# A planner's assumptions about landings, and where range checks may stand, in a one-core streaming encoder step

## The chip, the cores and the metric

The kernel runs on one core of a Trainium2 chip. A core has five engines that work side by side, each through its own instructions in a fixed order: TensorE (PE; its weight loads are shown apart as PEld) multiplies matrices, VectorE (DVE) and ScalarE (ACT) work elementwise, GpSimd (POOL) does the same more slowly, and SyncE (SP) issues DMAs. GpSimd also issues DMAs here. Instructions of different engines wait for each other through semaphores. The metric is the device time of one execution in microseconds.

## The reference, cut to what matters

One layer of an encoder is computed for 1024 tokens of a prompt and 8 x 16 sample tokens, 1152 tokens in all, with shared weights. From each token's normalised and modulated state `h` (width 1024) one wide projection makes everything else:

```python
mod = jax.nn.silu(c) @ w_ada + b_ada
shift, scale, gate = jnp.split(mod[:, None, :], 3, axis=-1)
h = rms_norm(x, norm_g) * (1 + scale) + shift
proj = h @ w_in
q, k, v, z_att, z_ssd, xbc, dt_raw, gates = jnp.split(proj, IN_SPLITS, axis=-1)
...
att_branch = (o_att.reshape(b, s, ATT_WIDTH) * jax.nn.silu(z_att)) @ w_att_proj
...
ssd_branch = y @ w_ssd_proj
g_att, g_ssd = jnp.split(gates, 2, axis=-1)
merged = jax.nn.sigmoid(g_att) * att_branch + jax.nn.sigmoid(g_ssd) * ssd_branch
out = x + gate * (merged @ w_out)
```

Branch A is attention over the own chunk of 64 and the 8 before it, branch B a gated state-space scan (SSD) over chunks of 64 with a short convolution ahead. Everything is float32.

## The kernel before, in words

**Precision.** Each float32 operand of a large product is split into two float16 halves: the high half is the rounded value, the low half what the rounding lost. A product is three float16 matmuls (high x high, high x low, low x high). `halves` (L691 to L698) does the split of a weight: ScalarE writes the high half (L697), VectorE the low half (L698). `level` (L685 to L689) is the range check of an operand: ScalarE squares it into a scratch tile and keeps the row means (L689, followed by a short read of the accumulator). Near the end `verdict` looks at these sums; its result decides whether the general kernel that follows in the program has to run (with these inputs it does not). So a range check has no reader for a long time, but it reads the raw weight, and the raw buffer cannot be loaded again before.

**Weights.** A weight piece of 512 KB (128 x 1024) is loaded by SyncE into one of three raw buffers (`w_ahead`, L675 to L681, the DMA is L679), rounded, checked, and its buffer is freed. `w_split` (L749) does this for one piece of a plain job, `quad_split` (L715) for one piece of a quad job. The projections of the last stage are quad jobs: the product of 2 x 2 blocks is made from seven products instead of eight (`quad_dense`), from four pieces. Two of them are input blocks (`in_quad_dram`), two are sums of blocks that `quad_sums` made earlier and stored in device memory (`sum_d`). Twenty quad jobs follow each other at the end.

**Stages.** 0 to about 58 us: norm, modulation, `h`, and the first projection. All of it is written out by hand: each instruction is `late`, which pins it behind the one before it on its engine. To about 600 us: attention, head pair by head pair, with the projections (`dense_tok` L1023 to L1025, `dense` L970 to L973) as filler for TensorE. To about 1265 us: the SSD scan with its projections. After that: the merge and the quad products (L876 to L878, evicted by L895 and L901, with conversions L2198 and L2200 of their operands).

**What sets the order.** The Python code writes instructions into a list. The class `Order` then plans an order for each engine, which the program keeps. It groups up to three matmuls to a unit, finds what each unit depends on, and simulates the five engines with assumed costs. At each step it takes the engine that can go on first, and on it, of the units that can start, the one earliest in the list, with two preferences. A unit is "sure" when its inputs have been there for a margin (300 ns on ScalarE and VectorE, 2500 ns after a DMA); sure ones go first. And a unit in the set `fill` counts as 600 places later in the list. A unit in `pinned` keeps its place behind its predecessor. The assumed landing of a DMA is in these lines (L386 to L388): `bus` is the end of the transfers so far, `lat` first the bytes by 360 GB/s (1456 ns for 512 KB), and at the end the time from issue to landing; a reader can start 60 ns after it.

```python
bus = max(t + 1400, bus) + lat
lanes[e][k] = bus + 700
lat = bus + 700 - t
```

Nothing in the plan is a clock on the chip: it only fixes the order, and on the chip each engine waits where an input is not there.

**Where the range checks of the first part stand.** `level(wraw[0].ap, SW, late)` (L1257), the three `level(b.ap, SW, late)` in `w_low2` (L1233), and the eight of `h` in `h_level` (L1437), which are neither pinned nor in `fill`.

Of the kernel before, what the change touches and what calls it, by code (L numbers as in the profile page):

```python
# [136 lines left out]
        self.arena.release(self.at)  # L137


class Order:  # L140


# [6 lines left out]
    FAST = 300  # L149
    SAFE_FAST = 200.0  # L150

    def __init__(self, tc, instructions, pinned, cuts, slow, fill, fast):
        self.tc, self.slow, self.fill, self.fast = tc, slow, fill, fast
        self.list = [x for x in instructions if x.opcode != "TilePoolBoundary"]
        self.pinned, self.cuts = pinned, cuts

    @staticmethod
    def engine(x):
# [74 lines left out]
    def build(self):  # L233

        units, self.of, last = [], {}, None
        for x in self.list:
            e = self.engine(x)
            if e == "PE":
                small = x.tile_size[0] * x.tile_size[1] < 16384
                out = x.outs[0].bass_ap.tensor.name  # L240
                key = (small, tuple(x.tile_size), "" if small else out)
                if last and last["key"] == key and x.name not in self.cuts and (small or len(last["ins"]) < 3):
                    last["ins"].append(x)
                    self.of[x.name] = last
                    continue
            u = {"eng": e, "ins": [x], "i": len(units), "pred": {}, "succ": [], "key": None}
            if e == "PE":
                u["key"] = key
                last = u
            units.append(u)  # L250
            self.of[x.name] = u
        self.units = units

        hist, prev = {}, {}
        tiles = {}
        for x in self.list:
            u = self.of[x.name]
            e = u["eng"]
            if x.name in self.pinned and e in prev and prev[e] is not u:
                u["pred"].setdefault(prev[e]["i"], 0)  # L260
            prev[e] = u
            acc = [(a, False) for a in x.ins if hasattr(a, "bass_ap")] + [(a, True) for a in x.outs if hasattr(a, "bass_ap")]
            for a, w in acc:
                t, name, r0, r1, c0, c1 = self.region(a)
                if not w and name.startswith("in_"):
                    continue
                tag = name.rstrip("0123456789_") if "PSUM" in str(t.space) else None
                if tag in self.SLOTS:
                    tiles.setdefault(name, [tag, []])[1].append(u["i"])
                    r0, r1, c0, c1, w = 0, 128, 0, 512, True  # L270
                for blk in range(c0 // 512, (c1 - 1) // 512 + 1):
                    h = hist.setdefault((name, blk), [])
                    keep = []
                    for v in h:
                        q0, q1, d0, d1, j, jw = v
                        if q0 < r1 and r0 < q1 and d0 < c1 and c0 < d1 and (w or jw):
                            if j != u["i"]:
                                k = 2 if jw and not w else 1
                                u["pred"][j] = max(u["pred"].get(j, 0), k)
                            if w and r0 <= q0 and q1 <= r1 and c0 <= d0 and d1 <= c1:  # L280
                                continue
                        keep.append(v)
                    b0, b1 = max(c0, 512 * blk), min(c1, 512 * blk + 512)
                    new = (r0, r1, b0, b1, u["i"], w)
                    if not keep or keep[-1] != new:
                        keep.append(new)
                    hist[name, blk] = keep
        for u in units:
            costs = [self.cost(x) for x in u["ins"]]
            u["busy"] = sum(c for c, _ in costs)  # L290
            u["fast"] = u["ins"][0].name in self.fast
            u["at"] = u["i"] + self.FILL * (u["ins"][0].name in self.fill) - self.FAST * u["fast"]
            u["lat"] = u["busy"] - costs[-1][0] + costs[-1][1]
            u["dma"] = u["ins"][0].opcode == "DMACopy" or u["ins"][0].opcode.startswith("DmaTranspose")
        self.tiles = tiles
        opener, members = {}, {}
        for name, (tag, us) in tiles.items():
            us = sorted(set(us))
            first = units[us[0]]
            first.setdefault("opens", []).append(name)  # L300
            if opener.get(tag, us[0]) != us[0]:
                first["pred"].setdefault(opener[tag], 0)
            opener[tag] = us[0]
            for j in us:
                units[j].setdefault("uses", []).append(name)
            members[name] = tag, us
            tiles[name] = [tag, len(us), 0.0]
        for name, (tag, us) in members.items():
            if any(x.name in self.cuts for x in units[us[0]]["ins"]) and tag == "g":
                for j in us[1:]:  # L310
                    if units[j]["eng"] == "PE":
                        for k, kind in units[j]["pred"].items():
                            if k not in us and k < us[0]:
                                units[us[0]]["pred"].setdefault(k, kind)
        for u in units:
            for j in u["pred"]:
                units[j]["succ"].append(u["i"])

    def run(self):
# [15 lines left out]
        def add(u):  # L335
            r = safe = 0.0
            for j, kind in u["pred"].items():
                v = units[j]
                if v["eng"] == u["eng"] and not v["dma"]:
                    t = finish[j] if kind == 2 and u["eng"] != "PE" else start[j]  # L340
                    m = 0.0
                else:
                    t = finish[j] + 60
                    m = self.SAFE_DMA if v["dma"] else self.SAFE_FAST if u["fast"] else self.SAFE[u["eng"]]
                r = max(r, t)
                safe = max(safe, t + m)
            u["r"], u["safe"] = r, safe
            ready[u["eng"]].append(u)

# [4 lines left out]
        while n < len(units):  # L354
            best = None
            for e in engines:
# [12 lines left out]
                t = max(free[e], min(c))  # L369
                if best is None or t < best[0]:  # L370
                    best = (t, e)
            assert best, ("no unit can go on", [(e, [(u["i"], u["ins"][0].name) for u in ready[e]][:4]) for e in engines])
            t, e = best
            can = [u for u in ready[e] if u["now"] <= t and u["i"] < low + self.AHEAD]
            sure = [u for u in can if u["sure"] <= t]
# [6 lines left out]
            if u["dma"]:  # L382
                k = nlane[e] % 8
                nlane[e] += 1
                t = max(t, lanes[e][k])
                bus = max(t + 1400, bus) + lat  # L386
                lanes[e][k] = bus + 700
                lat = bus + 700 - t  # L388
            busy = u["busy"]
            if e == "PE":  # L390
                g = u["key"][1]
# [34 lines left out]
def trunk_kernel(ctx: ExitStack, tc: tile.TileContext, h, again):  # L426
# [200 lines left out]
    dma = nc.sync.dma_start  # L627

    store = nc.gpsimd.dma_start
    pinned, cuts, slow, fill, fast = set(), set(), set(), set(), set()  # L630
    pinning = [True]

    def late(x):
# [81 lines left out]
    def quad_split(i):  # L715
# [23 lines left out]
        if j == 1:  # L739
            halves(a.r[:, :512], a.r[:, 512:], b.ap[:, 512:], SW)  # L740
        else:
            halves(a.r, bufs[n + 1].r, b.ap, SW)
        if j < 2:
            level(b.ap, SW)
        b.free()
# [3 lines left out]
    def w_split(i, keep=lambda x: x):  # L749

        if i in quads:
            return quad_split(i)
        n = len(jobs[i])
        w = parts[jobs[i][0]].shape[1]
        if i not in wsplit:
            lay = L_WD if n == 2 else L_W3 if n > 1 else L_W
            hi = alloc(lay, "w", n * w)
            try:
                lo = alloc(lay, "w", n * w)
            except NoSlot:  # L760
                hi.free()
                raise
            wsplit[i] = [hi, lo, 0]
        hi, lo, j = wsplit[i]
        w_ahead()
        b = wraw.pop(jobs[i][j])
        c = slice(j * w, (j + 1) * w)
        halves(hi.r[:, c], lo.r[:, c], b.ap[:, :w], SW, keep)
        level(b.ap[:, :w], SW, keep)
        b.free()  # L770
        wsplit[i][2] = j + 1
        w_ahead()
# [455 lines left out]
    def w_low2(j):  # L1228
# [1 line left out]
        b = wraw.pop(1 + j)  # L1230
        c = slice(j * 1024, (j + 1) * 1024)
        late(nc.vector.scalar_tensor_tensor(lo.r[:, c], b.ap, SW, hi.ap[:, c], ALU.mult, ALU.subtract))
        level(b.ap, SW, late)  # L1233
        b.free()


    for k in range(KT):
        if k == 0:
# [15 lines left out]
            mod_copy(2)  # L1254
            h_rest(1)
            w01_low(slice(256, 1024))
            level(wraw[0].ap, SW, late)  # L1257
            wraw.pop(0).free()
            z_mm(0, 0, hlo)
            mod_b(2)  # L1260
# [173 lines left out]
    def h_level():  # L1434
        for k in range(KT):
            yield from pause(6000)
            level(hhi[k].r, 1.0, kind="x")  # L1437

    urgent.append(ev_first())
    urgent.append(h_level())  # L1440
# [1023 lines left out]
    items.append((ssd_dense(1), [tile_loads(3, ("acc", acc_d, 0), ("gs", gate_d, 8), ("att", att_o, 0))], [], 0.5))  # L2464
    items.append((out_dense(), [], [], 0.5))
    run(items)
    order = Order(tc, list(nc.cur_bb.bb.instructions), pinned, cuts, slow, fill, fast)
    order.build()
    order.run()
    order.apply()  # L2470


# [1866 lines left out]
```

## Time and profile before

| | |
|---|---|
| median of 3 runs | 1724.09 us (1721.27 to 1725.7) |
| the profiled execution's own time | 1723.17 us |
| its span, first to last instruction | 1721.4 us |
| TensorE clock granted, mean | 0.998 |
| TensorE busy | 1678.6 us, 98% |
| VectorE, ScalarE, GpSimd busy | 1376.6, 1058.1, 369.1 us |

"Busy" of TensorE counts a matmul to its modelled end, and matmuls overlap: the row of a 384-column matmul says 327 ns, while in the order of time they start 0.16 us apart. Only where the profile shows idle time did TensorE stand. In the rows of waits, `ACT arena L697 <- DMA arena<-sum_d` reads: ScalarE was idle before an instruction of line 697 that writes the tile `arena` (nearly all of the on-chip memory is one tile), and what ended the wait was the landing of a DMA from `sum_d` into `arena`.

### The profile page before, as it was taken

The page shows a single profiled execution, that of the slowest core. Times are in us where ns is not written, and L with a number is a line of the kernel's source. Part 1 is how long each engine was busy: PE and PEld are TensorE (multiplying, and loading weights), DVE is VectorE, ACT ScalarE, POOL GpSimd, SP SyncE. Part 2 cuts the span into 40 slices and gives each one's busy share as a digit, 9 for nine tenths or more (in the row PEclk, how much of TensorE's full clock was granted, in tenths as well). Part 3 has the DMA queues.
Part 4 walks back from the last instruction along what each step waited for, and adds up shares of the span by engine and source line. Part 5 has one row for each costly group of instructions (what it writes and reads, how often), then busy time and mean ns, then how long its engine had stood idle before and what let it go on. Part 6 is the DMA issues. An engine that isn't in the chain of part 4 may idle for free. (4 is left out here: it accounts for less than half of the span.)

```text
span 1721.4 us, 36659 instructions
## 1 busy us (share of the span) xinstructions
PE 1678.6 (98%) x14265; PEld 1120.4 (65%) x14265; DVE 1376.6 (80%) x2539; ACT 1058.1 (61%) x2123; POOL 369.1 (21%) x640
## 2 busy tenths in 40 slices
PE   7999999999999999999999999999999999999998
PEld 3556565556565556666666666666657777777776
DVE  6458767878877888889988998997798677888973
ACT  8766556566565668457655765665379665774550
POOL 0133233135133111322321232232212101010000
PEclk9999999999999999999999999999999999999999
DMA  9248789797978687676858867788756866687661
GB/s 383 82 122 210 170 228 225 168 232 187 219 219 192 165 199 221 181 221 199 194 172 263 241 194 238 235 216 268 284 198 221 274 240 234 232 287 264 224 212 65
DMA packets 299249, 369.16 MB, mean 214 GB/s; under 512 B 211692, under 2 KB 213368, under 8 KB 299064
## 3 DMA queue, kind: packets, MB, share of 16 engines
q1 hardware_dynamic: 282040, 307.65, 64.0%
q0 software_dynamic: 17024, 59.06, 9.3%
q8 instruction: 114, 1.87, 0.5%
q14 instruction: 71, 0.58, 0.1%
HBM read 244.08 MB, written 74.06 MB: 185 GB/s over the span
## 5 line engine op out<-in xcount | busy, mean ns | idle before, releaser
L970 PE MATMUL d<-arena 128*128 128x384 f16 x1320 | 432.0, 327 | 4.4 <-DVE arena L1986 2.0
L973 PE MATMUL d<-arena 128*128 128x384 f16 x1320 | 431.5, 327 | 1.2 <-DVE arena L698 1.2
L971 PE MATMUL d<-arena 128*128 128x384 f16 x1320 | 431.3, 327 | 0.0
L689 ACT ACTIVATE arena<-arena 128x1024 bf16<-128x1024 f32 (+4 forms) x217 | 199.2, 918 | 130.1 <-DMA arena<-in_wall_dram 88.2
L698 DVE SCALAR_TENSOR_TENSOR arena<-arena 128x1024 f16<-128x1024 f32 (+2 forms) x157 | 181.8, 1166 | 61.0 <-ACT arena L697 60.5
L697 ACT ACTIVATE arena<-arena 128x1024 f16<-128x1024 f32 (+2 forms) x157 | 155.4, 994 | 83.2 <-DMA arena<-sum_d 40.5
L970 PEld LDWEIGHTS <-arena 128*128 128x128 f16 x1320 | 129.2, 98 | 90.9 <-issue 12.1
L1023 PE MATMUL d<-arena 128*128 128x384 f16 (+1 forms) x568 | 187.0, 329 | 0.0
L1024 PE MATMUL d<-arena 128*128 128x384 f16 (+1 forms) x568 | 186.3, 328 | 0.0
L1025 PE MATMUL d<-arena 128*128 128x384 f16 (+1 forms) x568 | 186.2, 328 | 0.0
L973 PEld LDWEIGHTS <-arena 128*128 128x128 f16 x1320 | 129.0, 98 | 87.8 <-DVE arena L698 1.9
L971 PEld LDWEIGHTS <-arena 128*128 128x128 f16 x1320 | 129.1, 98 | 82.5 <-issue 5.8
L1569 ACT ACTIVATE arena<-arena 128x640 f32<-128x640 f32 (+4 forms) x144 | 100.8, 701 | 63.4 <-DVE arena L1572 63.0
L877 PEld LDWEIGHTS <-arena 128*128 128x128 f16 x1120 | 109.3, 98 | 39.7 <-issue 12.2
L878 PEld LDWEIGHTS <-arena 128*128 128x128 f16 x1120 | 109.3, 98 | 32.4 <-issue 4.3
L876 PEld LDWEIGHTS <-arena 128*128 128x128 f16 x1120 | 109.4, 98 | 29.3 <-issue 1.5
L876 PE MATMUL d<-arena 128*128 128x288 f16 x400 | 114.5, 286 | 5.9 <-DVE arena L901 3.9
L876 PE MATMUL g<-arena 128*128 128x288 f16 x400 | 114.5, 286 | 1.2 <-DVE arena L901 1.2
L877 PE MATMUL g<-arena 128*128 128x288 f16 x400 | 114.5, 286 | 1.2 <-DVE arena L2200 1.2
L877 PE MATMUL d<-arena 128*128 128x288 f16 x400 | 114.5, 286 | 0.2 <-DVE arena L2200 0.2
L878 PE MATMUL g<-arena 128*128 128x288 f16 x400 | 114.5, 286 | 0.0
L878 PE MATMUL d<-arena 128*128 128x288 f16 x400 | 114.5, 286 | 0.0
(277 smaller groups left out, 3521.8 us busy)
## 6 DMA issues: line engine op xcount, KB each, us to landing
arena<-in_quad_dram SPq DMA_DIRECT2D x80, 512.0 KB, 7.0
arena<-in_wall_dram SPq DMA_DIRECT2D x77, 512.0 KB, 5.2
sum_d<-arena POOLq DMA_DIRECT2D x40, 512.0 KB, 4.9
arena<-sum_d SPq DMA_DIRECT2D x40, 512.0 KB, 4.9
arena<-acs_d SPq DMA_DIRECT2D x32, 576.0 KB, 6.2
arena<-in_kc_dram SPq DMA_DIRECT2D x64, 256.0 KB, 4.4
arena<-in_vc_dram SPq DMA_DIRECT2D x64, 256.0 KB, 3.6
arena<-in_wada_dram SPq DMA_DIRECT2D x24, 512.0 KB, 3.7
```

The costliest lines, as they stand in the source:

```text
L689: keep(nc.scalar.activation(junk[:, :n], x, AF.Square, scale=scale * n ** -0.5, accum_out=sums[:, c:c + 1]))
L697: keep(nc.scalar.activation(hi, x, AF.Copy, scale=scale))
L698: keep(nc.vector.scalar_tensor_tensor(lo, x, scale, hi, ALU.mult, ALU.subtract))
L876: nc.tensor.matmul(ps, wh, xh[:, c], start=first and k == 0, stop=False, skip_group_check=not first)
L877: nc.tensor.matmul(ps, wh, xl[:, c], start=False, stop=False, skip_group_check=not first)
L878: nc.tensor.matmul(ps, wl, xh[:, c], start=False, stop=k == 3, skip_group_check=not first)
L970: nc.tensor.matmul(ps, hi.r[:, wc], kh.r[:, tok], start=k == 0, stop=False)
L971: nc.tensor.matmul(ps, hi.r[:, wc], kl.r[:, tok], start=False, stop=False)
L973: nc.tensor.matmul(ps, lo.r[:, wc], kh.r[:, tok], start=False, stop=k == nk - 1)
L1023: nc.tensor.matmul(ps, kh.r[:, tok], wh, start=k == 0, stop=False)
L1024: nc.tensor.matmul(ps, kh.r[:, tok], wl, start=False, stop=False)
L1025: nc.tensor.matmul(ps, kl.r[:, tok], wh, start=False, stop=k == KT - 1)
```

## The change

Four things change in how the order is made. No operation of the computation is added or left out.

1. *Landings.* In the plan, a DMA issued after 600000 ns lands 1000 ns later than before. Its readers are planned by that; the transfers behind it on the bus are not moved.
2. *Patience.* A new set `patient` holds the rounding instructions (both halves) of a weight piece: in `quad_split` those of all pieces but the second, in `w_split` the rounding and the range check. If what such a unit waits for last in the plan is a DMA, it can start only 3000 ns after that, and is then sure at once.
3. *Free range checks.* The checks of the first weight pieces are no longer pinned; they and the checks of `h` are in `fill`.
4. *A stuck plan.* If no unit can go on, the matmuls that stand ready on TensorE are taken out of their groups and the plan is made again.

```diff
+class Stuck(Exception):
+    pass
...
-    def __init__(self, tc, instructions, pinned, cuts, slow, fill, fast):
-        self.tc, self.slow, self.fill, self.fast = tc, slow, fill, fast
+    def __init__(self, tc, instructions, pinned, cuts, slow, fill, fast, patient):
+        self.tc, self.slow, self.fill, self.fast, self.patient = tc, slow, fill, fast, patient
         self.list = [x for x in instructions if x.opcode != "TilePoolBoundary"]
-        self.pinned, self.cuts = pinned, cuts
+        self.pinned, self.cuts, self.apart = pinned, cuts, set()
...
-                if last and last["key"] == key and x.name not in self.cuts and (small or len(last["ins"]) < 3):
+                if last and last["key"] == key and x.name not in self.cuts and x.name not in self.apart and (small or len(last["ins"]) < 3):
...
+            u["patient"] = u["ins"][0].name in self.patient
...
                 r = max(r, t)
                 safe = max(safe, t + m)
+            if u["patient"] and any(units[j]["dma"] and finish[j] + 60 > r - 1 for j in u["pred"]):
+                r += 3000.0
+                safe = max(r, safe)
             u["r"], u["safe"] = r, safe
...
-            assert best, ("no unit can go on", [(e, [(u["i"], u["ins"][0].name) for u in ready[e]][:4]) for e in engines])
+            if not best:
+                raise Stuck([x.name for u in ready["PE"] for x in u["ins"]])
...
                 bus = max(t + 1400, bus) + lat
                 lanes[e][k] = bus + 700
-                lat = bus + 700 - t
+                lat = bus + 700 - t + (1000.0 if t > 600000.0 else 0.0)
...
         if j == 1:
             halves(a.r[:, :512], a.r[:, 512:], b.ap[:, 512:], SW)
         else:
-            halves(a.r, bufs[n + 1].r, b.ap, SW)
+            halves(a.r, bufs[n + 1].r, b.ap, SW, lambda x: patient.add(x.ins.name))
         if j < 2:
             level(b.ap, SW)
...
-        halves(hi.r[:, c], lo.r[:, c], b.ap[:, :w], SW, keep)
-        level(b.ap[:, :w], SW, keep)
+        k2 = lambda x: (keep(x), patient.add(x.ins.name))
+        halves(hi.r[:, c], lo.r[:, c], b.ap[:, :w], SW, k2)
+        level(b.ap[:, :w], SW, k2)
...
         late(nc.vector.scalar_tensor_tensor(lo.r[:, c], b.ap, SW, hi.ap[:, c], ALU.mult, ALU.subtract))
-        level(b.ap, SW, late)
+        level(b.ap, SW, lambda x: fill.add(x.ins.name))
...
-            level(wraw[0].ap, SW, late)
+            level(wraw[0].ap, SW, lambda x: fill.add(x.ins.name))
...
-            level(hhi[k].r, 1.0, kind="x")
+            level(hhi[k].r, 1.0, lambda x: fill.add(x.ins.name), kind="x")
...
-    order = Order(tc, list(nc.cur_bb.bb.instructions), pinned, cuts, slow, fill, fast)
-    order.build()
-    order.run()
+    order = Order(tc, list(nc.cur_bb.bb.instructions), pinned, cuts, slow, fill, fast, patient)
+    while True:
+        order.build()
+        try:
+            order.run()
+            break
+        except Stuck as x:
+            assert not order.apart.issuperset(x.args[0]), "no unit can go on"
+            order.apart.update(x.args[0])
     order.apply()
```

More of the change, by code (lines that the diff above doesn't have):

```diff
@@ L629, in trunk_kernel @@
     store = nc.gpsimd.dma_start
-    pinned, cuts, slow, fill, fast = set(), set(), set(), set(), set()
+    pinned, cuts, slow, fill, fast, patient = set(), set(), set(), set(), set(), set()
     pinning = [True]
```

## The prediction

> **What bounds the kernel now.** I read the page's head and DMA part first, then the busy times by stage, then who waited for whom.
>
> ```profile
> span 1721.4 us, 36659 instructions
> PE 1678.6 (98%) x14265; PEld 1120.4 (65%) x14265; DVE 1376.6 (80%) x2539; ACT 1058.1 (61%) x2123; POOL 369.1 (21%) x640
> ...
> arena<-in_quad_dram SPq DMA_DIRECT2D x80, 512.0 KB, 7.0
> arena<-in_wall_dram SPq DMA_DIRECT2D x77, 512.0 KB, 5.2
> ...
> arena<-sum_d SPq DMA_DIRECT2D x40, 512.0 KB, 4.9
> ```
>
> TensorE is busy for 1678.6 of 1721.4 us. The change neither adds nor removes a matmul, so all that it can win is in the 42.8 us in which TensorE is idle. The DMA rows matter too: a 512 KB weight piece lands 4.9 to 7.0 us after its issue in the median. The planner's own arithmetic (1400 + 1456 + 700 ns, in its code) puts it at 3.56 us when nothing else is in flight. So its plan believes in weights some 1.3 to 3.4 us before they are there.
>
> The stages, from the view of busy times by stretch (columns: stretch, its length, then busy time and instructions of TensorE, its weight loads, VectorE, ScalarE, GpSimd; clock; DMA):
>
> ```profile
> 20.00:60.00 40.00, 36.94 (x305) 21.04 (x298) 32.30 (x47) 38.88 (x71) 0.00 (x0) 1.00 0.81 310
> 60.00:100.00 40.00, 38.98 (x246) 23.91 (x244) 14.95 (x24) 30.80 (x67) 19.36 (x36) 1.00 0.19 61
> 100.00:600.00 500.00, 499.19 (x4947) 297.24 (x4946) 379.31 (x1019) 292.63 (x718) 150.70 (x268) 1.00 0.82 197
> 600.00:1265.00 665.00, 655.54 (x5237) 433.38 (x5235) 584.99 (x928) 403.34 (x749) 159.86 (x263) 1.00 0.75 218
> 1265.00:1700.00 435.00, 421.48 (x3380) 327.91 (x3379) 345.95 (x486) 278.76 (x505) 38.34 (x66) 1.00 0.69 234
> ```
>
> From 100 to 600 us TensorE idles 0.8 us: nothing to win there. From 600 to 1265 it idles 9.5 us, from 1265 to 1700 another 13.5 us, in the two early stretches 3.1 and 1.0 us. ScalarE is the pacing engine from 20 to 60 us (38.88 of 40). VectorE is at 88% from 600 to 1265.
>
> What ScalarE waits for in the two late stages (first two rows: 600 to 1265; the others: 1265 to 1700; microseconds, times, longest):
>
> ```profile
> ACT arena L689 <- DMA arena<-in_wall_dram: 87.4, 29, 9.8
> ACT arena L2013 <- DMA arena<-acs_d: 22.5, 10, 5.7
> ...
> ACT arena L697 <- DMA arena<-sum_d: 40.5, 20, 7.9
> ACT arena L697 <- DMA arena<-in_quad_dram: 23.4, 11, 4.9
> ACT arena L689 <- DMA arena<-in_quad_dram: 9.8, 3, 7.3
> ACT arena L2198 <- DMA gate_d<-arena: 3.3, 1, 3.3
> ```
>
> ScalarE works in the planned order. While it stands at a rounding (L697) or a range check (L689) whose weight has not landed, the evictions and conversions queued behind it stand too. The worst one, ScalarE's and then TensorE's rows in order of time:
>
> ```profile
> 1459.32 1.06 ACT L697 ACTIVATE arena<-arena 128x1024 f16<-128x1024 f32 x1 [7.90 <-DMA arena<-sum_d]
> ...
> 1461.76 0.67 ACT L2198 ACTIVATE arena<-arena 128x576 f16<-128x576 f32 x1
> ...
> 1462.47 0.28 PE L876 MATMUL s<-arena 128*128 128x288 f16 x1 [1.43 <-ACT arena L2198]
> 1463.27 0.28 PE L877 MATMUL s<-arena 128*128 128x288 f16 x1 [0.51 <-DVE arena L2200]
> ...
> 1466.86 0.28 PE L876 MATMUL s<-arena 128*128 128x288 f16 x1 [0.24 <-ACT arena L895]
> 1469.96 0.28 PE L877 MATMUL d<-arena 128*128 128x288 f16 x1 [0.25 <-DVE arena L2200]
> 1472.02 0.28 PE L877 MATMUL g<-arena 128*128 128x288 f16 x1 [1.17 <-DVE arena L2200]
> ```
>
> The rounding stands 7.90 us at a `sum_d` piece; the operand conversion L2198 behind it is late; TensorE loses 1.43 + 0.51 + 0.24 + 0.25 + 1.17 = 3.60 us.
>
> **The change, part by part.** *(a) Patience.* A rounding whose last condition is a landing is now planned no earlier than 3.06 us after that landing. It was allowed from 0.06 us on when ScalarE had nothing surer, and counted as sure from 2.5 us on. With the later landing of (b) a lone piece is planned to be rounded 3.56 + 1 + 3.06 = 7.6 us after its issue, above the medians of all three rows. No instruction is added; the engines only do other work first. Beside the 3.60 us, three stalls stand behind two more `sum_d` pieces, followed back from TensorE through the releases:
>
> ```profile
> 1476.28 1.06 ACT L697 ACTIVATE arena<-arena 128x1024 f16<-128x1024 f32 x1 [1.72 <-DMA arena<-sum_d]
> ...
> 1538.11 1.06 ACT L697 ACTIVATE arena<-arena 128x1024 f16<-128x1024 f32 x1 [1.17 <-DMA arena<-sum_d]
> ...
> 1480.06 0.28 PE L876 MATMUL d<-arena 128*128 128x288 f16 x1 [0.65 <-ACT arena L895]
> ...
> 1543.07 0.28 PE L876 MATMUL g<-arena 128*128 128x288 f16 x1 [1.08 <-DVE arena L901]
> 1545.73 0.28 PE L876 MATMUL d<-arena 128*128 128x288 f16 x1 [1.40 <-DVE arena L901]
> ```
>
> Together 3.60 + 0.65 + 1.08 + 1.40 = 6.7 us. I count all of it as won, between 0 and 6.7: with 4.06 us more distance only waits as long as the 7.90 survive, and shorter. The quad pieces read straight from the input get less. In `quad_split` the range check of the first two pieces carries no patience, and the second piece's rounding has none. The check can then stand first at the late landing, in the rounding's place.
>
> What the delay puts in danger: the raw buffer is held longer, and its next load is queued behind that on SyncE. There are three such buffers:
>
> ```profile
> 1290.00:1690.00 400.00, 70.23 (x75) 1.00 0.70 237
> ```
>
> 75 roundings in 400 us are 16.0 us for one turn of a buffer. A planned turn after the change is 7.6 us to the rounding, then 0.94 us for it (70.23/75) and about as much again for the low half and for the check: about 10.5. So over 5 us of cover remain; without it every 0.1 us more of a turn costs 400 x 0.1/16.0 = 2.5 us. I take 0.
>
> *(b) Landings 1 us later after 600 us.* Every DMA's readers are planned 1 us later; this also moves the reads of `acs_d`, `yb` and `gate_d`. TensorE's stalls that trace back to such a landing, or to a quad piece read from the input:
>
> ```profile
> 1209.93 0.32 PE L970 MATMUL d<-arena 128*128 128x384 f16 x1 [1.03 <-ACT arena L1919]
> ...
> 1370.64 0.28 PE L876 MATMUL d<-arena 128*128 128x288 f16 x1 [1.53 <-DVE arena L901]
> 1389.59 0.28 PE L876 MATMUL d<-arena 128*128 128x288 f16 x1 [0.78 <-DVE arena L901]
> 1528.60 0.28 PE L876 MATMUL d<-arena 128*128 128x288 f16 x1 [1.34 <-ACT arena L895]
> ```
>
> 4.7 us. Behind the second stands the wait of 3.3 us at `gate_d` above, which 1 us shortens but does not end; the worst at `acs_d` is 5.7, the mean 22.5/10 = 2.3. So I take half, 2.3, between 0 and 4.7.
>
> *(c) Free range checks in the first part.* Four checks of weights lose their pinned place in ScalarE's order and get low priority, the eight of h get low priority.
>
> ```profile
> L689 ACT ACTIVATE arena<-arena x7: 1043/1069/1175, 30.6 to 59.8; 128x1024 bf16<-128x1024 f32 x5, 128x1152 bf16<-128x1152 f16 x2
> ...
> PE g L1108 <- ACT arena L1127: 2.0, 4, 1.3
> PE g L1521 <- POOL arena L1501: 1.0, 1, 1.0
> ```
>
> The check at 30.6 us stands ahead of the copy L1127 for which TensorE then waits 1.3 us: won, 1.3. The three others stand where TensorE has the first projection to go on with, so they are worth nothing there. The four take 4 x 1.07 = 4.3 us out of ScalarE's tight stretch, and with the checks of h behind the evictions the chain to L1521 starts earlier: I take half of its 1.0. Sum 1.8, between 0 and 2.3. The raw buffers behind the checks come free later; TensorE's filler covers that, since the next weight is due only after the first projection.
>
> *(d) New stalls.* From 600 us on, every engine's order is drawn anew. The rest of the late idle time, 9.5 + 13.5 - 6.7 - 4.7 = 11.6 us, stands behind no landing that I could find; I let it recur at its size. What the new order adds lies between nothing and all that is won (10.8); no row prices it, and I take a quarter, 2.8, since the plan now errs less about landings.
>
> *(e) Splitting a group of matmuls where the planner is stuck:* 0, either not used or a change of order among the same matmuls.
>
> Sum: 6.7 + 2.3 + 1.8 - 2.8 = 8.0 us less. The profiled execution took 1723.17 us (span 1721.4 and 1.8 around it), which gives 1715.2; the median of the runs, 1724.09, lies 0.9 above it, so the forecast for a median is 1716.
>
> By the Trainium skill (DMA: Bandwidth & Descriptors, section "Anatomy of one DMA — SWDGE (gpsimd) path") a DMA takes about 2.0 us and its bytes over 436e3 per us, for 512 KB an estimate of 3.2 us. By that the planner's 3.56 us were enough, (a) and (b) would win nothing and the last rival below would be the likely one. The trace does not agree: 4.9 to 7.0 us.
>
> **The rivals.** *The gain is eaten (1722).* The new order's stalls cost all but 2 of the 10.8 us. For it: 11.6 us of idle time that has nothing to do with landings shows how easily a greedy order makes stalls. Against it: most of the won ones share one cause.
>
> *The change does not reach the waits (1720).* The wait only moves from the rounding to the unpatient check, and lateness is over 4 us where it hurts (7.9). Then (a) wins only the 3.1 us behind the two small latenesses, (c) 1.8, (b) 2.3 and (d) costs 2.8: 4.4 less, near 1720. For it: the 9.8 us at L689 from `in_quad_dram`. Against: `sum_d` pieces have the larger sum, and they are patient.
>
> *All landing stalls go (1706).* 6.7 + 4.7 + 2.3, and a third of the 11.6, which may be knock-on after all: 17.6 less, and nothing new. For it: the waits at landings are one family. Against: a third of them are behind plain landings, which move by 1 us alone.
>
> *VectorE's backlog (1732), slower.* Between 700 and 1100 us the low halves and everything fed by a landing move later in VectorE's order, where there is little room:
>
> ```profile
> 800.00:900.00 100.00, 98.49 (x787) 64.77 (x786) 88.57 (x135) 64.52 (x119) 30.60 (x47) 1.00 0.73 192
> 900.00:1000.00 100.00, 98.87 (x792) 66.91 (x792) 93.83 (x149) 65.30 (x123) 24.01 (x45) 1.00 0.83 242
> 1000.00:1100.00 100.00, 100.00 (x755) 66.34 (x754) 91.57 (x133) 57.55 (x103) 24.86 (x42) 1.00 0.70 223
> ...
> PE d L970 <- DVE arena L1986: 2.0, 1, 2.0
> ```
>
> Today one eviction in VectorE's queue comes 2.0 us late there. If each 100 us of the four such stretches had two of them, 16 us would be lost, less the 8 won: 8 more, 1732. It decides from the point at which VectorE passes some 94% of a stretch, since the 2.0 us fall at 900 us, where the stretch at 93.83 begins. Against it: the work on VectorE stays the same.
>
> *The raw buffers become the bound (1739).* If waiting in the queues stretches a turn from 10.5 to 16.6 us, the last stage grows by 0.6/16.0 of 400 us, 15 us. For it: reloads already wait for roundings. Against: the 5 us of cover.
>
> **How the numbers follow.** Forecast 1716: 0.43; eaten 0.16; not reached 0.11; all go 0.11; VectorE 0.13; buffers 0.06. The most that a measurement of this kernel can tell from no change is about 0.3%, 5.2 us. The forecast and "all go" are faster by more (0.54), "eaten" and "not reached" are within (0.27), the last two slower (0.19). The forecast's own range, from the bounds of (a) to (d), is 1709 to 1724. The range for 8 in 10 takes in "all go" and reaches to VectorE's backlog: 1704 to 1733.
>
> **What would show it.** Right: the rounding's wait for `sum_d` falls from 40.5 us to under 10, the check's wait for `in_wall_dram` from 87.4 to under 45, TensorE's idle time from 1265 to 1700 us from 13.5 to about 7, and the 1.3 us before L1108 is gone. Step (a) is wrong if ScalarE's waits shrink and TensorE's idle time stays; the check's wait for `in_quad_dram` above 20 us would show the moved wait. The forecast is wrong if TensorE's idle time from 600 to 1265 grows past 15 us behind VectorE, or if loads of raw pieces in the last stage follow each other at more than 5.3 us with TensorE waiting for low halves.

## The result, and the profile after

The changed kernel takes 1709.68 us in the median of six runs (1705.46 to 1716.62), the kernel before 1723.76 us beside it. The ratio is 0.9928, 95% interval 0.9904 to 0.9952: 14 us in the medians, 12.4 us by the ratio (8.3 to 16.5). The forecast was 1716 us, 8 us less than before. The profiled execution is the slowest of the six, 1716.62 us.

Lines of the changed kernel lie 9 to 10 below those of before: the rounding L697 and L698 is L706 and L707, the range check L689 is L698, `quad_dense`'s evictions L895 and L901 are L905 and L911. The head of its page and the busy times by stage, in the columns of the prediction:

```profile
span 1714.8 us, 36667 instructions
...
PE 1678.5 (98%) x14265; PEld 1124.5 (66%) x14265; DVE 1374.2 (80%) x2539; ACT 1058.8 (62%) x2123; POOL 393.4 (23%) x640
```

```profile
20.00:60.00 40.00, 36.24 (x306) 21.53 (x299) 31.96 (x47) 39.10 (x71) 0.00 (x0) 1.00 0.81 310
60.00:100.00 40.00, 36.94 (x222) 22.23 (x220) 12.66 (x21) 27.35 (x60) 18.13 (x30) 0.96 0.13 45
600.00:1265.00 665.00, 656.90 (x5255) 434.39 (x5250) 585.64 (x929) 401.38 (x741) 184.69 (x264) 0.99 0.74 220
1265.00:1700.00 435.00, 428.40 (x3440) 334.79 (x3439) 348.16 (x492) 282.99 (x514) 37.30 (x64) 0.99 0.67 233
```

TensorE's idle time from 1265 to 1700 us fell from 13.5 to 6.6 us, from 600 to 1265 us from 9.5 to 8.1. Early it rose: 60 to 100 us from 1.0 to 3.1, 20 to 60 us from 3.1 to 3.8. The clock column, 1.00 in all these stages before, shows 0.96 from 60 to 100 us and 0.99 in the two late stages: that is loss beside the idle time, and it comes back below.

ScalarE's waits at landings in the two late stages (first two rows 600 to 1265 us):

```profile
ACT arena L2023 <- DMA arena<-acs_d: 32.7, 12, 5.8
ACT arena L698 <- DMA arena<-in_wall_dram: 9.8, 4, 6.0
...
ACT arena L706 <- DMA arena<-in_quad_dram: 19.2, 8, 5.5
ACT arena L698 <- DMA arena<-in_quad_dram: 4.0, 4, 1.7
ACT arena L706 <- DMA arena<-sum_d: 3.7, 3, 1.7
```

The waits at `sum_d` went from 40.5 to 3.7 us, those of the check at `in_wall_dram` from 87.4 to 9.8. So nearly every sign that the prediction named came out as it said. The experiments show that the reason it gave for most of the gain was wrong all the same.

### The profile page after: what moved, and what is told of

Read it like the earlier page. It is cut to its first block, busy times and chain, and to the rows that moved or that the text cites. A ratio compares the mean times of both kernels' runs of the same rounds, so it can differ in the third digit from the quotient of the medians.

```text
span 1714.8 us, 36667 instructions
## 1 busy us (share of the span) xinstructions
PE 1678.5 (98%) x14265; PEld 1124.5 (66%) x14265; DVE 1374.2 (80%) x2539; ACT 1058.8 (62%) x2123; POOL 393.4 (23%) x640
## 4 chain that ended last, share of the span: by engine, by line
PE 79%; DVE 6%; ACT 5%; DMA 5%; issue 4%; POOL 1%; SPq 0%; POOLq 0%; DVEq 0%; ACTq 0%
PE d L980 10%; PE d L983 10%; PE d L981 10%; PE d L1033 6%; PE d L1034 5%; PE d L1035 5%; PE g L1639 2%; PE g L887 2%; PE g L888 2%; PE g L886 2%; PE d L886 2%; PE d L887 2%; PE d L888 2%; PE s L886 2%; DMA arena<-acs_d 2%
## 5 line engine op out<-in xcount | busy, mean ns | idle before, releaser
L698 ACT ACTIVATE arena<-arena 128x1024 bf16<-128x1024 f32 (+4 forms) x217 | 198.9, 917 | 51.8 <-DVE arena L2365 24.0
L707 DVE SCALAR_TENSOR_TENSOR arena<-arena 128x1024 f16<-128x1024 f32 (+2 forms) x157 | 181.2, 1163 | 38.2 <-ACT arena L706 36.4
L706 ACT ACTIVATE arena<-arena 128x1024 f16<-128x1024 f32 (+2 forms) x157 | 154.9, 991 | 27.5 <-DMA arena<-in_quad_dram 22.9
```

The costliest lines, as they stand in the source:

```text
L698: keep(nc.scalar.activation(junk[:, :n], x, AF.Square, scale=scale * n ** -0.5, accum_out=sums[:, c:c + 1]))
L706: keep(nc.scalar.activation(hi, x, AF.Copy, scale=scale))
L707: keep(nc.vector.scalar_tensor_tensor(lo, x, scale, hi, ALU.mult, ALU.subtract))
```

## The experiments

Each kernel is the changed one with parts taken back, or the one before with one thing altered. Ratios are to the kernel before, run beside it.

| kernel | ratio, 95% interval | median, us |
|---|---|---|
| landings + patience + free checks (the change) | 0.9928, 0.9904 to 0.9952 | 1709.7 |
| the same again | 0.9922, 0.9898 to 0.9945 | 1710.1 |
| free checks alone | 1.0026, 1.0004 to 1.0047 | 1725.8 |
| patience alone | 1.0009, 0.9985 to 1.0032 | 1726.9 |
| landings alone | 0.9921, 0.9895 to 0.9947 | 1709.9 |
| landings + patience | 0.9897, 0.9864 to 0.9931 | 1705.7 |
| the same again | 0.9893, 0.9867 to 0.9919 | 1705.2 |
| landings of raw weights alone | 0.9969, 0.9951 to 0.9987 | 1718.6 |
| landings of all but raw weights | 0.9927, 0.9910 to 0.9944 | 1711.6 |
| landings of GpSimd's DMAs alone | 1.0102, 1.0068 to 1.0136 | 1741.9 |
| landings 2 us later, alone | 1.0052, 1.0031 to 1.0072 | 1733.6 |
| before, ScalarE's assumed cost + 2 ns | 1.0005, 0.9990 to 1.0019 | 1724.1 |
| before, VectorE's assumed cost + 2 ns | 1.0048, 1.0029 to 1.0067 | 1731.2 |

### Patience alone

```diff
-                lat = bus + 700 - t + (1000.0 if t > 600000.0 else 0.0)
+                lat = bus + 700 - t
...
-        level(b.ap, SW, lambda x: fill.add(x.ins.name))
+        level(b.ap, SW, late)
```

(and the other two checks of the first part likewise.)

> Only the 3 us of patience for roundings. My theory: ScalarE's waits for sum_d fall from 40.5 us to under 10 and its range checks' waits for in_wall_dram from 87.4 to under 30; TensorE's idle time from 1265 us on falls from 13.5 us to about 8; 1716 us. The rival (lucky draw): the waits fall too, but TensorE's idle time needn't follow; 1710 to 1735.

Two of the waits fell much as both theories said, at `sum_d` from 40.5 to 11.9 us (I had expected under 10) and those of the check at `in_wall_dram` from 87.4 to 7.6. The check's wait at `in_quad_dram` rose from 9.8 to 21.4 us, and over 20 was the sign that the prediction had named for a wait that only moves. TensorE's idle time hardly fell. Waits of ScalarE (the first 600 to 1265 us, the others 1265 to 1700), then the busy times:

```profile
ACT arena L698 <- DMA arena<-in_wall_dram: 7.6, 7, 2.8
...
ACT arena L698 <- DMA arena<-in_quad_dram: 21.4, 8, 6.5
...
ACT arena L706 <- DMA arena<-sum_d: 11.9, 3, 6.0
```

```profile
600.00:1265.00 665.00, 653.43 (x5221) 432.50 (x5218) 582.06 (x923) 401.14 (x746) 172.24 (x262) 1.00 0.74 218
1265.00:1700.00 435.00, 424.02 (x3352) 329.38 (x3353) 345.09 (x486) 279.54 (x505) 35.80 (x66) 0.98 0.69 234
```

TensorE idles 11.0 us in the last stage against 13.5, with the clock at 0.98 instead of 1.00, and 11.6 against 9.5 in the stage before; no gain is left. At the place of the worst stall of before, and at the next one, stand in order of time:

```profile
1466.54 1.42 DVE L2296 SCALAR_TENSOR_TENSOR arena<-arena 128x1152 f32<-128x1152 f32 x1 [3.04 <-DMA arena<-y_d]
...
1469.28 0.28 PE L887 MATMUL d<-arena 128*128 128x288 f16 x1 [2.00 <-DVE arena L2210]
1471.35 0.28 PE L887 MATMUL g<-arena 128*128 128x288 f16 x1 [1.17 <-DVE arena L2210]
...
1539.68 1.06 ACT L698 ACTIVATE arena<-arena 128x1024 bf16<-128x1024 f32 x1 [3.63 <-DMA arena<-in_quad_dram]
...
1541.83 0.30 PE L886 MATMUL g<-arena 128*128 128x288 f16 x1 [1.83 <-ACT arena L706]
1543.09 0.30 PE L888 MATMUL g<-arena 128*128 128x288 f16 x1 [0.84 <-DVE arena L707]
```

The first stall now stands behind a plain landing (`y_d`, read by VectorE) that was next in line: in the kernel before, the same read stood 0.22 us at it, at 1466.35 us. Patience does nothing for it. In the second the unpatient check waits in the rounding's place, and TensorE waits for the roundings themselves, which stand behind it. Both had been named in the prediction. The moved wait was a rival there, in which (a) still wins 3.1 us; a plain landing that takes over the stall had no price.

### Landings alone

Patience off, checks pinned:

```diff
-            if u["patient"] and any(units[j]["dma"] and finish[j] + 60 > r - 1 for j in u["pred"]):
+            if False and any(units[j]["dma"] and finish[j] + 60 > r - 1 for j in u["pred"]):
```

> Only the landings that are planned 1 us later after 600 us. My theory: each of the 20 waits for sum_d gets about 1 us shorter (40.5 us to about 20), TensorE's idle time from 1265 us on falls to about 10 us; 1719 us. The rival (lucky draw): 1710 to 1735 with no relation to the waits.

All of the change's gain, 13.6 us by the ratio (9.1 to 18.1), with the waits at `sum_d` hardly changed:

```profile
ACT arena L706 <- DMA arena<-sum_d: 38.9, 16, 8.5
...
600.00:1265.00 665.00, 658.42 (x5273) 435.91 (x5268) 588.81 (x935) 405.70 (x748) 173.89 (x264) 1.00 0.74 222
1265.00:1700.00 435.00, 429.02 (x3470) 336.69 (x3469) 350.38 (x503) 280.70 (x508) 37.44 (x64) 1.00 0.68 232
```

TensorE's idle time in the last stage is 6.0 us, with 38.9 us of waits at `sum_d`; with patience alone it is 11.0 us, with 11.9. So the sum of ScalarE's waits at late weights does not set the end. My expectation for the waits (about 20 us) was wrong too.

### Free checks alone, and the change without them

Alone: both other parts off. Without: the three checks as before, the rest as changed.

> Only the free range checks of the first part; landings and patience as before. My theory: the late stages' waits at landings stay as before (ScalarE's rounding behind sum_d about 40 us in sum), TensorE's idle time from 1265 us on stays near 13.5 us, and the early stretch (20 to 100 us) loses about 3 us as in the changed kernel: 1727 us. The rival (the new order is a lucky draw, the cause of the gain is not the landings): any of the parts can bring the 14 us; this one alone could be 1710 to 1735.

> Landings and patience together, the range checks of the first part pinned as before. My theory: the early stretch is as before (TensorE idle 2.9 us from 20 to 60, 1.0 us from 60 to 100, no cold clock at 65 us), the late gain of the changed kernel stays: 1706 us, 3 to 4 us better than the changed kernel. The rival (lucky draw): without the free checks the late order is another one, so the late gain is lost in part: 1712 to 1725.

> Landings and patience without the free checks, beside the changed kernel on one chip: 1706 us. If the free checks cost what they cost alone, this is 3 to 5 us faster than the changed kernel; if not, the two are within 2 us.

> The changed kernel as it is: 1710 us, with a spread of some 5 us about it, since its stalls of 2.8 to 4 us sometimes cool the clock. The rival to the free checks' cost says within 2 us of the kernel without them.

Alone they cost 0.26%, 4.5 us (0.7 to 8.1). Beside each other on one chip the change takes 1710.05 us and the change without them 1705.23, 4.8 us less; in the first runs, not beside each other, it is 1709.68 against 1705.74. The intervals of the two ratios overlap both times, but the kernel without the checks is ahead both times. Where it goes: ScalarE in the kernel before, ScalarE in the changed kernel, TensorE in the changed kernel.

```profile
58.63 1.07 ACT L689 ACTIVATE arena<-arena 128x1024 bf16<-128x1024 f32 x1
...
59.83 1.16 ACT L689 ACTIVATE arena<-arena 128x1152 bf16<-128x1152 f16 x1
...
61.25 0.27 ACT L1465 ACTIVATE arena<-d 128x128 f32<-128x128 f32 x1
...
62.58 1.28 ACT L1311 ACT_TABLE_LOAD   x1
```

```profile
58.31 1.06 ACT L698 ACTIVATE arena<-arena 128x1024 bf16<-128x1024 f32 x1
...
59.50 1.16 ACT L698 ACTIVATE arena<-arena 128x1152 bf16<-128x1152 f16 x1
...
60.79 1.16 ACT L698 ACTIVATE arena<-arena 128x1152 bf16<-128x1152 f16 x1
...
62.06 1.28 ACT L1321 ACT_TABLE_LOAD   x1
...
64.00 0.29 ACT L1475 ACTIVATE arena<-d 128x128 f32<-128x128 f32 x1
...
64.34 0.32 PE L1033 MATMUL d<-arena 128*128 128x384 f16 x1 [2.82 <-ACT arena L1475]
...
65.77 0.53 PE L1035 MATMUL d<-arena 128*128 128x384 f16 x1
66.09 0.53 PE L1033 MATMUL d<-arena 128*128 128x384 f16 x1
...
68.94 0.33 PE L1033 MATMUL d<-arena 128*128 128x384 f16 x1
```

Three checks in a row and a table load stand ahead of the evictions (L1474, L1475) that free TensorE's accumulators. Before, two checks stood there, and the first evictions went ahead of the table load: what is new in front of them is one check, the table load and a copy behind it. `fill` gives low priority only among what can go on: where an eviction is not yet "sure" in the plan, a check that is ready goes first. That is how the rule reads; that it happened so in this plan is not shown. TensorE loses 2.82 us, and then its matmuls start 0.32 us apart instead of 0.16 until 68.9 us: the eleven steps from the start at 65.47 to the one at 68.94 us take 3.5 us instead of 1.8, another 1.7 us. The clock was granted at half there. With free checks alone the same 2.82 us stand there and the clock stays whole in the profiled execution, so the second part is not always paid. The change without the checks has neither.

### Which landings

The landings are made later for the loads of raw weight pieces alone, for all others alone, and for the DMAs that GpSimd issues alone (stores):

```diff
-                lat = bus + 700 - t + (1000.0 if t > 600000.0 else 0.0)
+                lat = bus + 700 - t + (1000.0 if t > 600000.0 and u["ins"][0].name in self.RAW else 0.0)
```

(`not in self.RAW`, and `e == "Pool"`, in the other two; `w_ahead` puts the names of its loads into `RAW`.)

> Landings 1 us later after 600 us, but for the loads of raw weight pieces alone; no patience, checks pinned. My theory now (patience alone won nothing although the waits at roundings went): the roundings' waits do not set TensorE's end, so this one wins little: 1718 to 1724, TensorE's idle time from 600 us on 18 us or more. The theory on record (roundings that stand at landings hold ScalarE): most of the 14 us, 1712.

> Landings 1 us later after 600 us for all DMAs but the loads of raw weight pieces (reads of the scan's sums, of stored gates and accumulators, stores whose buffers are reused). My theory now: these carry the gain: 1709 to 1714, TensorE's idle time from 600 us on about 12 us as with all landings. The theory on record: little, 1719 to 1724.

> Landings 1 us later after 600 us for the DMAs that GpSimd issues alone, nearly all of them stores (their landing frees a buffer, or makes a sum readable). If the stall of 3.1 us at 1260 us stands behind a store to sum_d whose buffer VectorE's L2245 writes again, it is gone here, with its cold clock: about 5 us won, 1718 to 1720, and the stalls from 1265 us on stay near 13 us. If that stall comes from the order alone, it stays: 1723.

The raw pieces win 5.3 us (2.2 to 8.4), all others 12.6 (9.7 to 15.5). The two sum to 17.9, more than the 13.6 of landings alone but within its interval (9.1 to 18.1). So the greater part goes with readers that my sum had left at 2.3 us. The times came as expected; TensorE's idle time from 600 us on did not, 15.6 us in the one profile (expected 18 or more) and 16.7 in the other (about 12). The profiled executions took 1715.45 and 1718.25 us, the fastest of the first kernel's runs and the slowest of the second's, so their idle times do not rank the two.

One stall can be followed to its landing through eleven kernels. In the kernel before it is the largest outside the start. VectorE's row, then ScalarE's, then TensorE's:

```profile
1252.62 1.36 DVE L2245 TENSOR_TENSOR arena<-arena 128x1152 f32<-128x1152 f16 x1 [1.67 <-DMA sum_d<-arena]
...
1258.70 1.35 DVE L2245 TENSOR_TENSOR arena<-arena 128x1152 f32<-128x1152 f16 x1
...
1260.15 0.68 ACT L689 ACTIVATE arena<-arena 128x576 bf16<-128x576 f32 x1 [0.17 <-DVE arena L2245]
...
1263.25 0.58 ACT L2381 ACTIVATE arena<-g 128x512 f32<-128x512 f32 x1
...
1263.88 1.06 PE L1108 MATMUL g<-arena 128*128 128x9 f32 x8 [3.08 <-ACT arena L2381]
...
1265.45 0.53 PE L970 MATMUL d<-arena 128*128 128x384 f16 x1
```

VectorE stands 1.67 us until a store to `sum_d` has landed and its buffer can be written. Everything behind comes late; ScalarE's four checks of VectorE's second result are ordered ahead of the eviction L2381, and TensorE stands 3.08 us and then runs at the half clock. Both the wait at `sum_d` and this stall (1.6 to 4.2 us) are there in the kernel before, with free checks alone, with patience alone, with raw landings alone and with both altered costs. Both are gone in the change and in the kernels with all landings, with landings and patience, with all but the raw, and with GpSimd's alone. So in all eleven the stall goes with how the stores' landings are planned, though the rest of the order differs among them too. With landings 2 us later VectorE again stands at such a store (3.25 us, at 1268 us), without this stall behind it. I had put this stall among those that "recur at their size".

GpSimd's landings alone lose 17.6 us in spite of that (11.7 to 23.4), far outside what I expected. New stalls stand behind it:

```profile
1024.29 0.69 ACT L2024 ACTIVATE arena<-arena 128x128 f32<-128x128 f32 x2 [13.84 <-DMA arena<-acs_d]
...
1028.03 0.48 PE L981 MATMUL d<-arena 128*128 128x384 f16 x1 [6.41 <-DVE arena L1997]
```

ScalarE stands 13.84 us at a read of `acs_d`. About half of that is not the landing: SyncE issues this load at 1017.28 us, 6.8 us after ScalarE began to wait, because it stood 5.0 us until a store to `y_d` had landed. The landing of the load, which this plan still put early, took the other 7 us.

### How much is in the draw

> Landings 2 us later after 600 us in place of 1 us, no patience, checks pinned. If the gain comes from planned landings that are nearer to the chip's, a lateness of 2 us keeps it or betters it: 1704 to 1711. If 1 us was a lucky draw: back towards before, 1715 to 1725.

> The kernel before, with the planner's assumed cost of every ScalarE instruction 2 ns higher: a change without meaning that draws the order anew. If landings are the cause of the gain: within 5 us of before (1719 to 1729), TensorE's idle time from 600 us on 20 to 27 us. If the gain is a lucky draw: such a change moves the time by 10 us and more in either direction.

> The same with VectorE: every assumed cost of the common forms 2 ns higher. If landings are the cause: 1719 to 1729. If the gain is a lucky draw: 10 us and more away in either direction.

Two changes without meaning make the kernel slower by 0.9 us (-1.7 to 3.3) and by 8.3 us (5.0 to 11.5). My 5 us bound for such a change was too narrow, though neither won anything. And 2 us later loses 9.0 us (5.3 to 12.4), where I expected it to keep the gain. Its two late stages, and what fills the second:

```profile
600.00:1265.00 665.00, 661.43 (x5283) 438.12 (x5282) 586.65 (x933) 400.00 (x738) 167.50 (x267) 1.00 0.76 221
1265.00:1700.00 435.00, 408.58 (x3251) 318.98 (x3250) 345.72 (x475) 285.47 (x511) 36.81 (x62) 0.96 0.66 228
...
1293.28 0.42 PE L886 MATMUL g<-arena 128*128 128x288 f16 x1 [10.49 <-ACT arena L706]
1300.44 0.42 PE L888 MATMUL g<-arena 128*128 128x288 f16 x1 [6.50 <-DVE arena L707]
```

From 600 to 1265 us TensorE idles 3.6 us, less than with 1 us later. Then, at the first quad products, it waits 17 us for two roundings that stand behind range checks and conversions on ScalarE and VectorE. The stages that were late are better; the place where the weights are wanted at once pays for it.

## Why the prediction was right or wrong

*Direction and range* held: 1709.68 lies in 1704 to 1733 and at the low edge of the forecast's own 1709 to 1724 (its terms sum to 13.7 us at most, so that edge is nearer to 1710). The size was 14.1 us, not 8.0. That the total came so near is luck: the term that was to bring most won nothing alone, one that was to bring a quarter won all, and (c) had the wrong sign. The bound, that only TensorE's idle time can be won, does not hold. Busy time is 1678.6 us before and 1678.5 in the change, but 1675.1 with landings alone (idle time 42.8 before, 33.0 there) and 1684.5 with patience alone. The clock is a part of that: up to 1700 us, patience alone ran 24 us of its profile at half rate, the kernel before 3.4. The rest was not followed.

*(a) Patience, "I count all of it as won", 6.7 us:* this step failed. Alone it moves the time by 0.09% (-0.15 to 0.32). It shortened ScalarE's waits, and the stalls passed to the next late landing at the same place and to the check without patience, as in the rival "the change does not reach the waits". On top of the landings the medians are 4 us lower (1705.7 against 1709.9), and the runs hardly overlap (1705.45 to 1708.08 against 1707.44 to 1711.14 on the same chip). So a gain there is likely, but it may belong to the other order that patience draws; that stays open. The error was to read a stall's last releaser as its cause, without asking which late input stood next. (A slip beside it: the distance that (a) and (b) add is 4.0 us, not 4.06, since 0.06 us were there before.)

*(b) Landings 1 us later, 2.3 us, at most 4.7:* right in sign, far too small. 13.6 us alone. The sum held only stalls that I had followed to a landing; the 3.08 us at 1260 us and the half clock behind it stood in the rest, because the wait at `sum_d` lies 11 us ahead of the stall, on another engine and two releases back.

*(c) Free checks, 1.8 us won:* wrong in sign, 4.5 us lost. The 1.3 us before L1108 was not won either: the four waits at that copy, 2.0 us in sum and at most 1.3 before, are 2.3 and at most 1.1 after. The new stall and these waits, from 20 to 100 us in the change:

```profile
PE d L1033 <- ACT arena L1475: 2.8, 1, 2.8
PE g L1118 <- ACT arena L1137: 2.3, 4, 1.1
```

"Low priority" was taken at its word; the plan's rule lets a ready check pass an eviction that is not yet sure.

*(d) New stalls, 2.8 us:* too small, and the clock was missing. The change has three of about 3 us or more, each followed by matmuls at half rate. The two late ones have grown from stalls at the same instructions before, 2.0 us at 900 us and 1.6 us at 1637 us:

```profile
903.66 0.48 PE L980 MATMUL d<-arena 128*128 128x384 f16 x1 [3.94 <-DVE arena L1996]
...
1628.31 0.28 PE L887 MATMUL s<-arena 128*128 128x288 f16 x1 [3.09 <-DVE arena L2210]
```

(the third is the 2.82 us at 61 us). VectorE's backlog, the slower rival, is real at 900 us, once instead of eight times, and not by the mark of 94%: from 900 to 1000 us VectorE is busy for 86.25 of 100 us there. The rival of the raw buffers did not come as such: in the change TensorE waits 0.3 us in all for a low half from 600 us on. With 2 us roundings came too late, through the queues of ScalarE and VectorE.

*The signs* named in advance (waits at `sum_d` under 10, at `in_wall_dram` under 45, idle time in the last stage about 7 us) all appeared, except the 1.3 us. They could not tell (a) from (b), because both were in the change.

*The estimate of 3.2 us* from the Trainium skill was set beside loads that SyncE issues, while the section that the prediction names is about DMAs of GpSimd. The trace does not agree on that path either: GpSimd's 512 KB stores to `sum_d` land 4.9 us after their issue in the median before.

*What stays open:* whether landings nearer to the chip's are good as such. For it: 1 us alone repeats the gain, each of its two parts wins, and the stall at 1260 us goes with the stores' landings in eleven kernels. Against it: 2 us and the stores alone lose, and a change without meaning moved the time by 8 us. Only two such changes were tried, and both were slower; they do not show how often a draw wins 14 us. Part of the 14 us may be a good draw of the order; how large a part was not measured.

## What to carry to other kernels

A wait that ends just before a stall is not yet its cause: ask which other input of the stalled chain was late as well, and take the parts of a change apart before believing signs that all of them share. Where an order comes from a greedy planner, run one or two changes without meaning first, so that a gain can be held against the spread of such draws. Work with no reader that is put at low priority still goes ahead of whatever the planner does not hold to be certain; here one more range check and a table load ahead of the evictions cost more than was won.

## What the runs showed of the hardware

In these traces TensorE's clock is granted in full or at half, and it falls to half for 3.4 or 6.8 us at a time (once for 20.5 us, around the stalls of 10.49 and 6.50 us with landings 2 us later; stretches that the end of the kernel cuts off are not counted). A stretch of 3.4 us costs up to 1.7 us of matmul time, as in the rows at 65 us above, one of 6.8 us up to 3.4. The fall need not wait for the end of the stall: in the change it begins 1.1 us after the stall of 2.82 us, and about 2 us before the end of the one of 3.94 us.

The length of the stall alone does not decide. The 2.82 us at 64 us were followed by the fall in the change, and not with free checks alone; stalls of 1.6 to 2.5 us were followed by it in some profiles and not in others. From 20 us on, every stall of 2.9 us and more in the profiles has it. The Trainium skill (TensorE: Matmul & The Clock Gate, section "Part 1: The HAM clock gate") gives an idle window of about 3.4 us and half rate. The half rate agrees, 0.32 us between starts instead of 0.16; the stalls that sufficed can be shorter here. For a stall near 3 us a price is the idle time and, in most of these profiles, 1.7 to 3.4 us more.
